# Gated unit of the experts: clamps moved to GpSimd, one eviction to ScalarE, the slots' small work rearranged

## The chip, the cores and the metric

One NeuronCore of a Trainium2 chip runs the program. The metric is the device time of one execution in microseconds (us); less is better.

## The reference

The reference is a whole small model on 512 tokens of width 1024: a first block (four token mixers, then 32 experts of which each token takes 4) and a second block of two layers. The change touches the experts alone. For one expert and its rows, with `w_gu` 1024 x 2048 and `w_down` 1024 x 1024, in fp32:

```
hg, hl = split(x @ w_gu[e] + b_gu[e])
hg = min(hg, 7);  hl = clip(hl, -7, 7)
y  = (hg * sigmoid(1.702 * hg) * (hl + 1)) @ w_down[e] + b_down[e]
out[token] += gate[token, e] * y
```

## The kernel before

The experts run one after the other (`for e in range(k.n_exp)`, up to L1538 and on). Each has 96 slots (`NS`): a token's rank in the expert is its slot. For each expert there are four steps.

**Slots** (`slots`, L1393 to L1414, called by `first`, L1468, two experts ahead). The narrow matrix `sel` (L1397) carries the bias rows. For each of the four groups of 128 tokens a one-hot matrix `o1` of 128 x 96 is made by comparing ranks with a row of slot numbers (VectorE, L1401), and a small matmul with it (L1402) puts token number, presence and gate of each slot into one PSUM tile. VectorE copies that to `sl` (L1404) and makes from it, in five operations on 96 x 1 elements (L1409 to L1413), the row `ix` to gather, the row `dx` to add to, and the gate `gc`.

**Rows** (`rows`, L1416, one expert ahead). GpSimd gathers the tokens' rows into `xg` by an indirect DMA (L1419). TensorE transposes them; `transposed` (L1224) evicts each transposed tile twice: ScalarE writes the high part (L1231), VectorE the low part (L1232).

**Main** (`main`, L1425). A fp32 product is made of three matmuls on split operands (high x high, high x low, low x high; L1148 to L1150). A weight piece of 128 x 2048 (1 MB) is loaded by SyncE's queue (L1204) into one of nine raw buffers; ScalarE copies it to the rounded high part `wh` (L1213), VectorE subtracts to get the low part `wl` (L1214). There are four buffers each of `wh` and `wl`. An expert has 12 pieces, eight for `w_gu` and four for `w_down`. The 2048 columns of `w_gu` are taken in two halves (`q`), each of which has a gate tile `pp[0]` and a linear tile `pp[1]` of 96 x 512 in PSUM, two pieces each. Once a half's tiles are there, the gated unit (L1440 to L1448) runs:

```
V.tensor_scalar(hg, pp[0], 7.0, None, op0=OP.min)
ACT.activation(sg, hg, AF.Sigmoid, scale=1.702)
V.tensor_scalar(hl, pp[1], 7.0, -7.0, op0=OP.min, op1=OP.max)
G.tensor_mul(hg, hg, sg)
V.scalar_tensor_tensor(hl, hl, 1.0, hg, op0=OP.add, op1=OP.mult)
last = transposed(hl, hT[0][:, 4 * q:4 * q + 4], hT[1][:, 4 * q:4 * q + 4])
```

(V is VectorE, ACT is ScalarE, G is GpSimd.) `hg`, `hl` and `sg` have one buffer each. The transposed `hT` (high part on ScalarE, low part on VectorE) is the operand of the down projection.

**Result.** ScalarE evicts the two halves of the product with the gate as scale (L1463), and GpSimd adds the rows to `h_d` by an indirect DMA (L1464, the scatter).

What runs in which order: each engine works its own queue strictly in order. The queues are laid out when the program is built, by the framework's planner, which goes through time in its own estimate of durations and takes for each engine what is ready there, earlier source lines first. So the order of a queue is not that of the source, and it changes when durations or dependences change. `issue_after` (used around the loads of the first experts and the extra work between experts) pins single orders; none of these lines is touched.

Of the kernel before, what the change touches and what calls it, by code (L numbers as in the profile page):

```python
# [8 lines left out]
F32 = mybir.dt.float32  # L9
F32R = mybir.dt.float32r  # L10
BF = mybir.dt.bfloat16
I32 = mybir.dt.int32
U32 = mybir.dt.uint32
AF = mybir.ActivationFunctionType
OP = mybir.AluOpType
# [5 lines left out]
NCH = 4  # L21
# [303 lines left out]
def tile_pool(tc, **kw):  # L325
    if kw.get("space") != bass.MemoryType.DRAM:
        kw["reuse_waits"] = "tile"
    return tc.tile_pool(**kw)
# [726 lines left out]
NS = 96  # L1055
# [90 lines left out]
def mm3(PE, out, a, b, start, stop):  # L1146

    PE.matmul(out, a[0], b[0], start=start, stop=False)  # L1148
    PE.matmul(out, a[0], b[1], start=False, stop=False)  # L1149
    PE.matmul(out, a[1], b[0], start=False, stop=stop)  # L1150


def block1_ffn(k, mix, wo, es_mix, b2):


    nc, tc, A = k.nc, k.tc, k.A
    V, ACT, G, PE = nc.vector, nc.scalar, nc.gpsimd, nc.tensor
    es, es_b, es_p, es_x = ExitStack(), ExitStack(), ExitStack(), ExitStack()
    with es:
# [7 lines left out]
        cons, sm = pool_x("fcons"), pool_x("sm")  # L1167
# [4 lines left out]
        iota, pidx = cst2[:, 0:128], cst2[:, 128:129]  # L1172
# [4 lines left out]
        Rm = cons.tile([128, NCH, N_EXP], F32, name="Rm")  # L1177
        aux = cons.tile([128, NCH, N_EXP, 6], BF, name="aux")
        dslot = cons.tile([128, 1], F32, name="dslot")
# [56 lines left out]
        with tile_pool(tc, name="w1", bufs=1) as w1:  # L1236
# [30 lines left out]
            eye3 = sm.tile([128, 32], F32, name="eye3")  # L1267
# [121 lines left out]


        with tile_pool(tc, name="ex", bufs=1) as ex:

            def slots(rm, ax, idc, eng=G):  # L1393


                sel = sm.tile([128, NS], BF, name="sel", bufs=3)
                eng.tensor_copy(sel, idc.to_broadcast([128, NS]))  # L1397
                pt = bank("tr", (NS, 512))
                for t in range(NCH):
                    o1 = sm.tile([128, NS], BF, name="o1", tag="o1", bufs=4)  # L1400
                    V.tensor_scalar(o1, iota[:, 0:NS], rm(t), None, op0=OP.is_equal)  # L1401
                    PE.matmul(pt[:, 0:6], o1, ax(t), start=t == 0, stop=t == NCH - 1)  # L1402
                sl = sm.tile([NS, 6], F32, name="sl", bufs=2)
                V.tensor_copy(sl, pt[:, 0:6])  # L1404
                tk = sm.tile([NS, 2], F32, name="tk", bufs=2)
                ix = sm.tile([NS, 1], I32, name="ix", bufs=3)
                dx = sm.tile([NS, 1], I32, name="dx", bufs=4)
                gc = sm.tile([NS, 1], F32, name="gc", bufs=4)
                V.scalar_tensor_tensor(tk[:, 0:1], sl[:, 1:2], 128.0, sl[:, 0:1], op0=OP.mult, op1=OP.add)  # L1409
                V.tensor_copy(ix, tk[:, 0:1])  # L1410
                V.tensor_scalar(tk[:, 1:2], sl[:, 2:3], -1.0, 1.0, op0=OP.mult, op1=OP.add)
                V.scalar_tensor_tensor(dx, tk[:, 1:2], dslot[:NS], tk[:, 0:1], op0=OP.mult, op1=OP.add)
                V.scalar_tensor_tensor(gc, sl[:, 3:4], sl[:, 4:5], sl[:, 5:6], op0=OP.add, op1=OP.add)  # L1413
                return sel, dx, gc, ix  # L1414

            def rows(sel, dx, gc, ix):  # L1416

                xg = ex.tile([NS, D], F32, name="xg", bufs=1)
                gathers.append(G.indirect_dma_start(out=xg, out_offset=None, in_=x1_d,  # L1419
                                                    in_offset=bass.IndirectOffsetOnAxis(ap=ix[:, :1], axis=0)))  # L1420
                xT = [ex.tile([128, 8, NS], F32R, name="xT%d" % i, bufs=2) for i in range(2)]
                transposed(xg, xT[0], xT[1])
                return sel, dx, gc, xT

            def main(st, wg, wd, mid=None, keep=None):  # L1425

                sel, dx, gc, xT = st
                hT = [ex.tile([128, 8, NS], F32R, name="hT%d" % i, bufs=1) for i in range(2)]
                for q in range(2):
                    pp = []  # L1430
                    for gl in range(2):
                        p = bank("gu", (NS, 512))
                        PE.matmul(p, sel, bias[:, 1024 * gl + 512 * q:1024 * gl + 512 * q + 512], start=True, stop=False)
                        for kh in range(2):
                            h, l = wg(4 * q + 2 * gl + kh)
                            for j in range(4):
                                a = 4 * kh + j
                                mm3(PE, p, (xT[0][:, a], xT[1][:, a]), (h[:, j], l[:, j]), False, a == 7)
                        pp.append(p)
                    hg = ex.tile([NS, 512], F32, name="hg", bufs=1)  # L1440
                    hl = ex.tile([NS, 512], F32, name="hl", bufs=1)
                    sg = ex.tile([NS, 512], F32, name="sg", bufs=1)
                    V.tensor_scalar(hg, pp[0], 7.0, None, op0=OP.min)
                    ACT.activation(sg, hg, AF.Sigmoid, scale=1.702)  # L1444
                    V.tensor_scalar(hl, pp[1], 7.0, -7.0, op0=OP.min, op1=OP.max)
                    G.tensor_mul(hg, hg, sg)  # L1446
                    V.scalar_tensor_tensor(hl, hl, 1.0, hg, op0=OP.add, op1=OP.mult)
                    last = transposed(hl, hT[0][:, 4 * q:4 * q + 4], hT[1][:, 4 * q:4 * q + 4])  # L1448
                with tc.issue_after(last.ins):
                    res = mid() if mid else None  # L1450
                y = None if keep else ex.tile([NS, D], F32, name="y", bufs=1)
                py = [bank("py", (NS, 512)) for _ in range(2)]
                for kh in range(2):
                    for n in range(2):
                        h, l = wd(2 * kh + n)
                        for j in range(4):
                            a = 4 * kh + j
                            mm3(PE, py[n], (hT[0][:, a], hT[1][:, a]), (h[:, j], l[:, j]), a == 0, a == 7)
                if keep:
                    keep(py, dx, gc)  # L1460
                    return res
                for n in range(2):
                    ACT.activation(y[:, 512 * n:512 * n + 512], py[n], AF.Copy, scale=gc)  # L1463
                G.indirect_dma_start(out=h_d, out_offset=bass.IndirectOffsetOnAxis(ap=dx[:, :1], axis=0),  # L1464
                                     in_=y, in_offset=None, compute_op=OP.add)
                return res

            first = lambda e: slots(lambda t: Rm[:, t, e:e + 1], lambda t: aux[:, t, e], eye3[:, e:e + 1], G if e else V)  # L1468
            def embedding():

                pe_ = xp.tile([128, NCH, D], F32, name="pe_", tag="x")
# [31 lines left out]
            def load_h(t):  # L1503
                nc.sync.dma_start(hs[t], h_d[128 * t:128 * t + 128])
# [27 lines left out]
            sl = [first(0)]  # L1532
# [21 lines left out]
            with tc.If(nov > 0):  # L1554
                with tc.For_i(0, nov, 1) as b:
                    e = nc.values_load(tble[0:1, bass.ds(b, 1)], min_val=0, max_val=N_EXP - 1)
                    rme = ex.tile([128, NCH, 1], F32, name="rme", bufs=1)
                    axe = ex.tile([128, NCH, 1, 6], BF, name="axe", bufs=1)
                    ide = ex.tile([128, 1], F32, name="ide", bufs=1)
                    jc = ex.tile([128, 1], F32, name="jc", bufs=1)  # L1560
                    V.tensor_copy(rme, Rm[:, :, bass.ds(e, 1)])
                    V.tensor_copy(axe, aux[:, :, bass.ds(e, 1)])
                    V.tensor_copy(ide, eye3[:, bass.ds(e, 1)])
                    V.tensor_copy(jc, tblj[:, bass.ds(b, 1)])
                    V.tensor_scalar(rme, rme, jc, None, op0=OP.subtract)
                    slow = lambda w: lambda i: unit(w[bass.ds(e, 1), i].rearrange("o p a b -> (o p) a b"), sx)
                    main(rows(*slots(lambda t: rme[:, t], lambda t: axe[:, t, 0], ide)), slow(A["wgu"]), slow(A["wdn"]))
                for t in range(2):
                    load_h(t)
            es_b.close()  # L1570
# [5 lines left out]
        with tile_pool(tc, name="pl", bufs=1) as pl:  # L1576
# [39 lines left out]
            for t in range(NCH):  # L1616
# [6 lines left out]
                for n in range(2):  # L1623
# [7 lines left out]
                    sg = pl.tile([128, 512], F32, name="sg", tag="sg", bufs=2)  # L1631
# [44 lines left out]
class B2:  # L1676
# [7 lines left out]
    def bank(self, tag, shape=(128, 512)):  # L1684
        n = int(np.prod(shape[1:]))
        a = self.ps.tile([128, 512], F32, name=tag, tag=tag, bufs={"gu": 4, "py": 2, "tr": 2}[tag])[:shape[0], :n]
        return a.rearrange("p (a b) -> p a b", a=shape[1]) if len(shape) == 3 else a
# [839 lines left out]
```

## Time and profile before

| | |
|---|---|
| median of 3 runs | 3156.93 us (3152.36 to 3159.75) |
| the profiled execution | 3154.36 us, its span 3152.6 us |
| busy share of the span | TensorE 94%, VectorE 68%, ScalarE 48%, GpSimd 26% |
| moved by the transfers | 582.12 MB, mean 185 GB/s |
| granted TensorE clock, mean | 0.968 |

The profile is one execution. Names: PE is TensorE's matmuls, PEld its weight loads, DVE is VectorE, ACT ScalarE, POOL GpSimd, SP SyncE (SPq its queue, which issues the loads). L1214 is line 1214 of the kernel. In a timeline the first column is the start in us from the span's start, the second the duration in us; `x2` after a line means two of the same merged, and the brackets hold the idle time ahead of the first and what ended it. The names of tiles are cut (`o` is `o1`). The experts lie between about 473 and 1690 us; before them are the mixers, after them the second block.

### The profile page before, as it was taken

Reading aid. Unit: us, or ns where it says so; the run is one execution under the profiler, and the core shown is the slowest. Engines: PE = TensorE matmul, PEld = TensorE weight load, DVE = VectorE, ACT = ScalarE, POOL = GpSimd, SP = SyncE. Lnnn points to the kernel's source line nnn. Section 1 sums busy time; section 2 is a strip of 40 time slices with the busy share of each in tenths; the row PEclk is TensorE's granted clock in tenths of the full one; section 3 lists DMA queues with packets and bytes.
Section 4 is the critical chain, followed back from the end, with each engine's and each line's share of the span. In section 5 each row is a group of like instructions: output and inputs, shape, how many; then the busy total and the mean of one; then the engine's idle time right before and its main releaser. Section 6 shows DMA issues by size and latency. Waiting matters only on the chain. (4 is left out here: it accounts for less than half of the span.)

```text
span 3152.6 us, 45612 instructions
## 1 busy us (share of the span) xinstructions
PE 2975.8 (94%) x18295; PEld 2471.6 (78%) x18295; DVE 2152.6 (68%) x3044; ACT 1521.8 (48%) x1838; POOL 831.8 (26%) x543
## 2 busy tenths in 40 slices
PE   6899879999999999999999999999999899999997
PEld 4799666666666666666666898999999799899997
DVE  4756679899999998899998756644233846834234
ACT  4421437776666666666665643342223534432222
POOL 1210333543333333233323310320103401310104
PEclk8999889999999999999999988999999999999998
DMA  3211368999999998899996211122222211232221
GB/s 122 74 35 35 109 248 324 342 369 351 350 351 346 348 351 323 336 341 345 349 350 226 79 58 41 57 91 82 93 94 80 97 41 46 76 108 87 99 78 52
DMA packets 106280, 582.12 MB, mean 185 GB/s; under 512 B 13080, under 2 KB 13736, under 8 KB 56048
## 3 DMA queue, kind: packets, MB, share of 16 engines
q1 hardware_dynamic: 94976, 541.12, 46.4%
q0 software_dynamic: 10896, 37.52, 4.5%
q8 instruction: 145, 2.38, 0.3%
q10 hardware_dynamic: 192, 0.52, 0.1%
q14 instruction: 71, 0.58, 0.1%
HBM read 560.17 MB, written 18.94 MB: 184 GB/s over the span
## 5 line engine op out<-in xcount | busy, mean ns | idle before, releaser
L1214 DVE TENSOR_TENSOR wl<-w,wh 128x2048 fp32r<-128x2048 f32 (+1 forms) x398 | 900.4, 2275 | 63.9 <-ACT wh L1213 63.7
L1213 ACT ACTIVATE wh<-w 128x2048 fp32r<-128x2048 f32 (+1 forms) x410 | 726.1, 1805 | 64.8 <-PE gu L1150 42.4
L1796 PE MATMUL gu<-hh,w 128*128 128x256 f32 (+2 forms) x1552 | 455.7, 294 | 10.4 <-ACT hh L2494 10.4
L1797 PE MATMUL gu<-hl,w 128*128 128x256 f32 (+2 forms) x1552 | 451.9, 291 | 2.0 <-DVE hl L2496 1.3
L1798 PE MATMUL gu<-hh,w 128*128 128x256 f32 (+2 forms) x1552 | 449.5, 290 | 1.8 <-DVE w L1142 1.8
L1149 PE MATMUL gu<-wl,xT 128*96 128x512 f32 x1024 | 416.8, 407 | 19.4 <-DVE wl L1214 18.5
L1148 PE MATMUL gu<-wh,xT 128*96 128x512 f32 x1024 | 410.8, 401 | 0.0
L1150 PE MATMUL gu<-wh,xT 128*96 128x512 f32 x1024 | 405.4, 396 | 0.0
L1142 DVE TENSOR_TENSOR w<-w 128x1024 fp32r<-128x1024 f32 (+1 forms) x190 | 237.6, 1251 | 238.0 <-ACT w L1141 237.8
L1141 ACT ACTIVATE w<-w 128x1024 fp32r<-128x1024 f32 (+1 forms) x194 | 201.2, 1038 | 259.8 <-PE gu L2320 84.6
L1796 PEld LDWEIGHTS gu<-hh,w 128*128 128x128 f32 x1552 | 301.4, 194 | 13.3 <-ACT hh L2494 12.0
L1797 PEld LDWEIGHTS gu<-hl,w 128*128 128x128 f32 x1552 | 300.0, 193 | 5.7 <-DVE hl L2496 3.9
L1798 PEld LDWEIGHTS gu<-hh,w 128*128 128x128 f32 x1552 | 300.8, 194 | 3.2 <-DVE w L1142 2.6
L1149 PEld LDWEIGHTS gu<-wl,xT 128*96 128x96 f32 x1024 | 165.5, 162 | 133.7 <-DVE wl L1214 70.7
L1446 POOL TENSOR_TENSOR hg<-hg,sg 96x512 f32<-96x512 f32 x64 | 170.8, 2669 | 284.8 <-ACT sg L1444 284.7
L2305 POOL TENSOR_TENSOR al<-fs,ah 128x528 fp32r<-128x528 f32 (+1 forms) x44 | 76.8, 1745 | 610.4 <-ACT ah L2304 610.4
L1148 PEld LDWEIGHTS gu<-wh,xT 128*96 128x96 f32 x1024 | 165.4, 162 | 69.5 <-ACT xT L1231 0.2
L1150 PEld LDWEIGHTS gu<-wh,xT 128*96 128x96 f32 x1024 | 165.7, 162 | 60.8
L1149 PE MATMUL py<-wl,hT 128*96 128x512 f32 x512 | 208.0, 406 | 1.8 <-DVE wl L1214 0.3
L1148 PE MATMUL py<-wh,hT 128*96 128x512 f32 x512 | 202.1, 395 | 1.7 <-ACT wh L1213 1.0
L1150 PE MATMUL py<-wh,hT 128*96 128x512 f32 x512 | 202.5, 398 | 0.0
L1464 POOL DMA_INDIRECT h_d<-y,dx x31 | 128.8, 4154 | 191.1 <-ACT y L1463 185.9
(707 smaller groups left out, 6413.7 us busy)
## 6 DMA issues: line engine op xcount, KB each, us to landing
w<-in_wgu SPq DMA_DIRECT2D x255, 1024.0 KB, 6.8
w<-in_wdn SPq DMA_DIRECT2D x127, 1024.0 KB, 7.6
w<-in_w SPq DMA_DIRECT2D x88, 512.0 KB, 4.3
w<-in_w2f SPq DMA_DIRECT2D x43, 512.0 KB, 4.6
w<-in_w22a SPq DMA_DIRECT2D x32, 512.0 KB, 4.4
w<-in_w1f SPq DMA_DIRECT2D x18, 512.0 KB, 3.6
w<-in_w2o SPq DMA_DIRECT2D x16, 512.0 KB, 4.3
w<-in_w22b SPq DMA_DIRECT2D x16, 384.0 KB, 4.3
```

What stands on the lines that cost most here:

```text
L1141: nc.scalar.activation(h, w, AF.Copy)
L1142: (eng or nc.vector).tensor_sub(l, w, h.bitcast(F32))
L1148: PE.matmul(out, a[0], b[0], start=start, stop=False)
L1149: PE.matmul(out, a[0], b[1], start=False, stop=False)
L1150: PE.matmul(out, a[1], b[0], start=False, stop=stop)
L1213: ACT.activation(h[:, j], w[:, j], AF.Copy)
L1214: (early or V).tensor_sub(l[:, j], w[:, j], h[:, j].bitcast(F32))
L1446: G.tensor_mul(hg, hg, sg)
L1464: G.indirect_dma_start(out=h_d, out_offset=bass.IndirectOffsetOnAxis(ap=dx[:, :1], axis=0), in_=y, in_offset=None, compute_op=OP.add)
L1796: PE.matmul(p, w[0][:, kk], x[0][:, kk, c], start=kk == ks[0], stop=False)
L1797: PE.matmul(p, w[0][:, kk], x[1][:, kk, c], start=False, stop=False)
L1798: PE.matmul(p, w[1][:, kk], x[0][:, kk, c], start=False, stop=kk == ks[-1])
```

## The change

The gate branch: ScalarE takes the sigmoid straight from PSUM; GpSimd limits the result from above with the constant sigmoid(1.702 x 7), made once in `smax` (the sigmoid is monotone, so this equals the sigmoid of the clamped value); VectorE clamps the PSUM value and multiplies in one operation. The linear branch: ScalarE copies the PSUM tile to SBUF, GpSimd clamps it on both sides in place, VectorE's last product stays. In the slots, one operation compares all four groups (`o1` has one buffer now, of 4 x 96); the matmuls read its quarters. For all experts but the first, `sl` is evicted by ScalarE and the five narrow operations run on GpSimd.

```diff
@@ -1389,6 +1389,9 @@
 
 
         with tile_pool(tc, name="ex", bufs=1) as ex:
+            smax = sm.tile([128, 1], F32, name="smax", bufs=1)
+            G.memset(smax, 7.0)
+            ACT.activation(smax, smax, AF.Sigmoid, scale=1.702)
 
             def slots(rm, ax, idc, eng=G):
 
@@ -1396,21 +1399,25 @@
                 sel = sm.tile([128, NS], BF, name="sel", bufs=3)
                 eng.tensor_copy(sel, idc.to_broadcast([128, NS]))
                 pt = bank("tr", (NS, 512))
+                o1 = sm.tile([128, NCH, NS], BF, name="o1", tag="o1", bufs=1)
+                V.tensor_tensor(o1, iota[:, 0:NS][:, None, :].to_broadcast([128, NCH, NS]),
+                                rm.to_broadcast([128, NCH, NS]), op=OP.is_equal)
                 for t in range(NCH):
-                    o1 = sm.tile([128, NS], BF, name="o1", tag="o1", bufs=4)
-                    V.tensor_scalar(o1, iota[:, 0:NS], rm(t), None, op0=OP.is_equal)
-                    PE.matmul(pt[:, 0:6], o1, ax(t), start=t == 0, stop=t == NCH - 1)
+                    PE.matmul(pt[:, 0:6], o1[:, t], ax(t), start=t == 0, stop=t == NCH - 1)
                 sl = sm.tile([NS, 6], F32, name="sl", bufs=2)
-                V.tensor_copy(sl, pt[:, 0:6])
+                if eng is V:
+                    V.tensor_copy(sl, pt[:, 0:6])
+                else:
+                    ACT.activation(sl, pt[:, 0:6], AF.Copy)
                 tk = sm.tile([NS, 2], F32, name="tk", bufs=2)
                 ix = sm.tile([NS, 1], I32, name="ix", bufs=3)
                 dx = sm.tile([NS, 1], I32, name="dx", bufs=4)
                 gc = sm.tile([NS, 1], F32, name="gc", bufs=4)
-                V.scalar_tensor_tensor(tk[:, 0:1], sl[:, 1:2], 128.0, sl[:, 0:1], op0=OP.mult, op1=OP.add)
-                V.tensor_copy(ix, tk[:, 0:1])
-                V.tensor_scalar(tk[:, 1:2], sl[:, 2:3], -1.0, 1.0, op0=OP.mult, op1=OP.add)
-                V.scalar_tensor_tensor(dx, tk[:, 1:2], dslot[:NS], tk[:, 0:1], op0=OP.mult, op1=OP.add)
-                V.scalar_tensor_tensor(gc, sl[:, 3:4], sl[:, 4:5], sl[:, 5:6], op0=OP.add, op1=OP.add)
+                eng.tensor_scalar(tk[:, 0:1], sl[:, 1:2], 128.0, sl[:, 0:1], op0=OP.mult, op1=OP.add)
+                eng.tensor_copy(ix, tk[:, 0:1])
+                eng.tensor_scalar(tk[:, 1:2], sl[:, 2:3], -1.0, 1.0, op0=OP.mult, op1=OP.add)
+                eng.tensor_scalar(dx, tk[:, 1:2], dslot[:NS], tk[:, 0:1], op0=OP.mult, op1=OP.add)
+                eng.tensor_scalar(gc, sl[:, 3:4], sl[:, 4:5], sl[:, 5:6], op0=OP.add, op1=OP.add)
                 return sel, dx, gc, ix
 
             def rows(sel, dx, gc, ix):
@@ -1440,10 +1447,12 @@
                     hg = ex.tile([NS, 512], F32, name="hg", bufs=1)
                     hl = ex.tile([NS, 512], F32, name="hl", bufs=1)
                     sg = ex.tile([NS, 512], F32, name="sg", bufs=1)
-                    V.tensor_scalar(hg, pp[0], 7.0, None, op0=OP.min)
-                    ACT.activation(sg, hg, AF.Sigmoid, scale=1.702)
-                    V.tensor_scalar(hl, pp[1], 7.0, -7.0, op0=OP.min, op1=OP.max)
-                    G.tensor_mul(hg, hg, sg)
+
+                    ACT.activation(sg, pp[0], AF.Sigmoid, scale=1.702)
+                    G.tensor_scalar(sg, sg, smax[:NS], None, op0=OP.min)
+                    V.scalar_tensor_tensor(hg, pp[0], 7.0, sg, op0=OP.min, op1=OP.mult)
+                    ACT.activation(hl, pp[1], AF.Copy)
+                    G.tensor_scalar(hl, hl, 7.0, -7.0, op0=OP.min, op1=OP.max)
                     V.scalar_tensor_tensor(hl, hl, 1.0, hg, op0=OP.add, op1=OP.mult)
                     last = transposed(hl, hT[0][:, 4 * q:4 * q + 4], hT[1][:, 4 * q:4 * q + 4])
                 with tc.issue_after(last.ins):
@@ -1465,7 +1474,7 @@
                                      in_=y, in_offset=None, compute_op=OP.add)
                 return res
 
-            first = lambda e: slots(lambda t: Rm[:, t, e:e + 1], lambda t: aux[:, t, e], eye3[:, e:e + 1], G if e else V)
+            first = lambda e: slots(Rm[:, :, e:e + 1], lambda t: aux[:, t, e], eye3[:, e:e + 1], G if e else V)
             def embedding():
 
                 pe_ = xp.tile([128, NCH, D], F32, name="pe_", tag="x")
@@ -1564,7 +1573,7 @@
                     V.tensor_copy(jc, tblj[:, bass.ds(b, 1)])
                     V.tensor_scalar(rme, rme, jc, None, op0=OP.subtract)
                     slow = lambda w: lambda i: unit(w[bass.ds(e, 1), i].rearrange("o p a b -> (o p) a b"), sx)
-                    main(rows(*slots(lambda t: rme[:, t], lambda t: axe[:, t, 0], ide)), slow(A["wgu"]), slow(A["wdn"]))
+                    main(rows(*slots(rme, lambda t: axe[:, t, 0], ide)), slow(A["wgu"]), slow(A["wdn"]))
                 for t in range(2):
                     load_h(t)
             es_b.close()
```

## Rows read from the trace of the kernel before

**Rows 1.** Busy time in stretches of 38.70 us: engine (instructions), granted clock, DMA share, GB/s

```profile
677.40:716.10 38.70, 38.34 (x179) 26.57 (x178) 38.48 (x35) 28.56 (x23) 15.88 (x5) 1.00 0.99 371
...
832.20:870.90 38.70, 37.76 (x170) 25.03 (x171) 35.43 (x33) 26.02 (x20) 13.21 (x5) 1.00 0.97 354
```

**Rows 2.** Timeline of DVE, 842 to 881 us: start, duration, operation

```profile
842.21 0.27 DVE L1401 TENSOR_SCALAR o<-fcst,Rm 128x96 bf16<-128x96 f32 x1 [0.55 <-PE tr L1402]
...
843.10 2.28 DVE L1214 TENSOR_TENSOR wl<-w,wh 128x2048 fp32r<-128x2048 f32 x1
...
851.27 0.69 DVE L1443 TENSOR_SCALAR hg<-gu 96x512 f32<-96x512 f32 x1 [0.66 <-PE gu L1150]
851.88 2.28 DVE L1214 TENSOR_TENSOR wl<-w,wh 128x2048 fp32r<-128x2048 f32 x1
854.53 2.93 DVE L1214 TENSOR_TENSOR wl<-w,wh 128x2048 fp32r<-128x2048 f32 x1 [0.37 <-ACT wh L1213]
857.38 0.68 DVE L1445 TENSOR_SCALAR hl<-gu 96x512 f32<-96x512 f32 x1
858.17 0.69 DVE L1447 SCALAR_TENSOR_TENSOR hl<-hl,hg 96x512 f32<-96x512 f32 x1
...
862.07 2.29 DVE L1214 TENSOR_TENSOR wl<-w,wh 128x2048 fp32r<-128x2048 f32 x1 [0.54 <-ACT wh L1213]
864.28 0.68 DVE L1443 TENSOR_SCALAR hg<-gu 96x512 f32<-96x512 f32 x1
...
880.59 0.27 DVE L1401 TENSOR_SCALAR o<-fcst,Rm 128x96 bf16<-128x96 f32 x1 [0.57 <-PE tr L1402]
```

**Rows 3.** Timeline of PEld (weight loads), from 870.60 us on

```profile
870.60 0.16 PEld L1150 LDWEIGHTS py<-wh,hT 128*96 128x96 f32 x1
870.83 0.16 PEld L1148 LDWEIGHTS py<-wh,hT 128*96 128x96 f32 x1
...
871.98 0.54 PEld L1230 LDWEIGHTS tr<-fcst,hl 96*128 96x128 f32 x4
872.46 0.16 PEld L1150 LDWEIGHTS py<-wh,hT 128*96 128x96 f32 x1
```

**Rows 4.** Waits, 600 to 1600 us: us in total, times, longest

```profile
ACT hT L1231 <- PE tr L1230: 152.7, 47, 4.6
...
ACT sg L1444 <- DVE hg L1443: 80.9, 46, 3.1
PEld gu L1149 <- DVE wl L1214: 64.7, 108, 1.7
```

**Rows 5.** Timeline of ACT, 852 to 864 us

```profile
852.06 0.63 ACT L1444 ACTIVATE sg<-hg 96x512 f32<-96x512 f32 x1 [2.81 <-DVE hg L1443]
852.60 3.71 ACT L1213 ACTIVATE wh<-w 128x2048 fp32r<-128x2048 f32 x2
859.74 0.49 ACT L1231 ACTIVATE hT<-tr 128x384 fp32r<-128x384 f32 x1 [3.44 <-PE tr L1230]
860.13 3.71 ACT L1213 ACTIVATE wh<-w 128x2048 fp32r<-128x2048 f32 x2
```

**Rows 6.** Timeline of POOL, 846 to 855 us

```profile
846.52 5.45 POOL L1464 DMA_INDIRECT h_d<-y,dx  x1 [0.30 <-issue]
852.77 2.54 POOL L1446 TENSOR_TENSOR hg<-hg,sg 96x512 f32<-96x512 f32 x1 [0.81 <-ACT sg L1444]
```

**Rows 7.** Single lines on POOL: ns min/median/max, first and last start us, forms

```profile
L1446 POOL TENSOR_TENSOR hg<-hg,sg x64: 1287/2547/7555, 477.5 to 1685.1; 96x512 f32<-96x512 f32 x64
...
L1397 POOL CAST sel<-eye x31: 262/267/4967, 402.3 to 1542.2; 128x96 bf16<-128x96 f32 x31
...
L528 POOL MEMSET SC<- x1: 529/529/529, 4.7 to 4.7; 128x512 f32 x1
```

**Rows 8.** Groups by line, 600 to 1600 us: count, busy us, mean ns, idle before

```profile
L1401 DVE TENSOR_SCALAR o<-fcst,Rm 128x96 bf16<-128x96 f32 x104 | 35.0, 370 | 9.0 <-PE tr L1402 9.0
...
L1480 ACT ACTIVATE pe__10029<-gu 128x512 f32<-128x512 f32 x8 | 4.8, 595 | 9.5 <-PE gu L1150 9.5
```

**Rows 9.** Transfers: a 10 us stretch (columns as rows 1), and SPq's waits, 600 to 1600

```profile
1310.00:1320.00 10.00, 9.70 (x47) 6.57 (x46) 9.70 (x8) 5.48 (x5) 0.00 (x0) 1.00 1.02 423
...
SPq L1204 <- DVE wl L1214: 844.9, 301, 12.3
```

## The prediction

> **What bounds the kernel now.** I read the busy time by stretches first, because the change touches one stage, the 32 experts from about 473 to 1690 us. Each row of [rows 1] is 38.70 us, about one expert. In the later one TensorE shows 37.76 us busy, VectorE 35.43, ScalarE 26.02, and the transfers 0.97; no engine has the stage to itself, but VectorE and TensorE are both nearly full. The next expert is a copy of it: the pair of one-hot operations that starts at 842.21 starts again at 880.59 [rows 2], so one expert takes 38.38 us.
>
> TensorE's own work is less. A triple of matmuls shows weight loads 0.23 us apart, and four transposes push the next load back by about half a microsecond [rows 3]. One expert has 12 weight pieces of 12 matmuls, four bias matmuls and 16 transposes: 144 x 0.23 + 4 x 0.23 + 4 x 0.5 = 36.0 us. The other 2.4 us are bubbles; 64.7 us of waits in 1000 us stand against VectorE's low parts "wl" [rows 4]. So 2.4 us an expert, some 75 us over 31 experts, is the most that any relief of the helpers can bring before TensorE itself is the bound.
>
> Why does VectorE come late when it is not full? Its stretch from 851.27 to 864.28 is one half of an expert, 13.01 us [rows 2], and with ScalarE's queue beside it [rows 5] it reads as a closed chain: clamp "hg" 851.27, sigmoid 852.06, weight copy 852.60, low part "wl" 854.53, clamp "hl" 857.38, product 858.17, transposes on TensorE, eviction hT 859.74, weight copy 860.13, low part 862.07, and the next clamp at 864.28. The steps are 0.79 + 0.54 + 1.93 + 2.85 + 0.79 + 1.57 + 0.39 + 1.94 + 2.21 = 13.01. TensorE needs 48 x 0.23 + 2 x 0.23 + 0.5 = 12.0 for a half. ScalarE waits in its queue for hT while weight copies stand behind it: that wait, 152.7 us, is the largest of an engine that matters, and the one for "hg" is 80.9 [rows 4]. The chain through ScalarE's in-order queue, not VectorE's sum, sets the half.
>
> GpSimd is idle most of the time, yet not free to use: its product of two tiles of 512 elements takes 2.54 us at 852.77 [rows 6], against a minimum of 1.29 [rows 7]. It starts while VectorE's low part of 851.88 runs, ends 1.15 us after that has ended, and the next low part takes 2.93 instead of 2.28 [rows 2]. The two take turns: GpSimd waits for a VectorE operation on two SBUF tiles, then holds the next one up by 0.65. A one-operand cast does the same: 0.26 us at best, 4.97 at worst [rows 7].
>
> **The change, part by part.** *Gate branch.* The sigmoid no longer waits for VectorE's clamp: the link of 0.79 drops from the chain, and ScalarE's weight copy with it comes 0.7 us earlier. The clamp by GpSimd and the product on VectorE follow off the chain, but the product, 0.69 by the one at 858.17 [rows 2], takes the place that the clamp had in VectorE's queue, and what stands behind it (the low part that TensorE wants next) waits if GpSimd is late. GpSimd is late if the scatter of the previous expert's result is still there, 5.45 us from 846.52 [rows 6]: it ended at 851.97, 0.1 us before the sigmoid began at 852.06 [rows 5]. Cover is thus thin once per expert.
>
> *Linear branch.* VectorE's clamp, a link of 0.79, becomes an eviction by ScalarE, 0.60 by the nearest row [rows 8], with 0.07 to its semaphore, then a GpSimd clamp and another semaphore of 0.1. *A clamp on GpSimd* does not occur in this trace with one operand on 96x512. From below I bound it by the fill of 128x512, 0.53, which reads nothing, from above by the two-operand minimum of 1.29 [rows 7]; I take 0.8, nearer to the fill because one operand is read instead of two. The linear link is then 0.67 + 0.9 = 1.57 instead of 0.79. [...]
>
> Per half, with the order of the queues kept, the chain is 13.01 - 0.79 + 0.78, plus up to 0.6 where the gate's product now stands ahead of a low part: 13.0 to 13.6, no gain.
>
> *VectorE's load.* One operation of 0.6 goes per half, and the 0.65 of being held up goes; two clamps of 0.8 now take turns with its low parts. That is -1.25 + 1.6, no relief worth the name: GpSimd's work is paid in VectorE's time where the clamps meet low parts.
>
> *Slots.* Four one-hots become one of 384 elements, and six narrow operations leave VectorE. From 842.21 to 843.10 two one-hots and the six narrow ones take 0.89 [rows 2]; the other two one-hots take half of 0.74, the mean of one being 0.37 [rows 8]. One operation of 4 x 96 costs 0.27 to 0.69 (one narrow one-hot up to the 512-element product), I take 0.45. So VectorE gets back 0.8 us per expert. What it loses is five narrow GpSimd operations at 0.1 to 0.26 each; at worst each is held up by a low part, 5 x 2.28 = 11.4 us of GpSimd's queue, ahead of gather and scatter. The gather it feeds is one expert ahead, so this costs nothing unless it pushes the scatter past the sigmoid as above; then the price is at most the 2 to 3 us by which the gate's clamp is late. ScalarE gains an eviction of 96x6, 0.2, in slack. The single one-hot buffer and the constant at the start are worth nothing each.
>
> **Where the gain comes from.** The chain closes only because hT stands in ScalarE's queue ahead of the second pair of weight copies (859.74 before 860.13). The new hT becomes ready 0.8 us later; the queue order is fixed when the program is built, in order of estimated readiness, so I expect the planner to put one more weight copy ahead of hT, and its low part ahead of the hT low part on VectorE. Then 0.39 + 1.94 + 2.21 no longer follow the transposes, the chain is open, and TensorE's 12.0 per half binds. With VectorE as full as before I take half of the 1.0: 0.5 x 62 halves = 31 us, and 5 us for the slots: 36 us. Against the profiled execution's 3154.4 that is 3118; the median of the runs is 2.6 above, so **3121 us**. The same sum at a clamp of 1.29 loses 2 x 0.49 x 62 = 61 at worst, at 0.53 it gains up to 33; with half of either on the path, this case alone spans 3090 to 3150.
>
> **Rivals.** *TensorE fully fed:* 2.4 x 31 = 74 us, 3083. For it: between 677.40 and 716.10 the transfers ran at 371 GB/s and TensorE was 38.34 us busy of 38.70 [rows 1]. Against: VectorE was 38.48 busy there, and its load does not fall.
>
> *The order stays, or the clamps simply move the time:* 13.0 for 13.01, nothing measurable (under 0.2%, about 6 us, cannot be told from no change): 3157. For it: the turns that GpSimd and VectorE take.
>
> *Slower, by the linear clamp held up.* If the planner lets the next low part run while ScalarE evicts the second branch, the clamp waits for it, up to 2.28 us, as the product did at 852.77, and the transposes, hT and what stands behind hT come that much later. If a weight copy that TensorE needs is still behind hT, the half is about 15 us: 2.1 x 62 = 130, 3287; if that holds in one half of each expert, 3222. It decides when the hold exceeds the 1.0 us of slack per half. For it: the product met a low part in nearly every half (median 2.55 against 1.29 [rows 7]); against: the planner sees the longer chain.
>
> *The transfers bind.* In the repeating expert the loads move 354 GB/s with a share of 0.97 [rows 1]; if that is all they give, an expert stays at 38.4 us and nothing is gained: 3157. Against: 371 GB/s over a whole such stretch [rows 1], 423 over 10 us, and the loads wait 844.9 us of 1000 for low parts that free their buffers [rows 9]; they follow, they don't lead. [...]
>
> **Chances.** Forecast 0.44, fully fed 0.08 (faster, 0.52 together); transfers 0.03 and no net change 0.14 (same, 0.17); slower 0.31. The range runs from the fully fed 3080 to 3205, which takes in the cheap part of the slower case; the likeliest case's own range is 3090 to 3150.
>
> **What would show it.** Right: ScalarE's wait for the transposes of hT well under 152.7 us in the same 1000 us, three or more weight copies between sigmoid and hT, VectorE waiting more for GpSimd but TensorE less for "wl", an expert in about 37.2 us. Step by step: one-operand clamps of 0.5 to 1.3 us when not held up, one one-hot near 0.45. Wrong: clamps of 2.5 us and above between ScalarE's eviction and the second product, with waits of TensorE for "wl" grown; or a product of the gate that stands waiting behind the scatter, with low parts late behind it.

## The result, and the profile after

The changed kernel takes 3246.69 us (median of 4, 3233.50 to 3257.98) against 3158.34 for the kernel before: a ratio of 1.0278, 95% interval 1.0246 to 1.0311. It is slower by 88 us, outside the range of the prediction.

The profiled execution took 3242.62 us, 88.3 more than that of before. Between the first and the last gate operation of VectorE lie 1297.3 us, where 1210.5 lay before; so nearly all of it, 86.8 us, is in the experts, some 2.8 us an expert. The first rows are VectorE's timeline of the changed kernel, two experts.

```profile
969.46 0.56 DVE L1403 TENSOR_TENSOR o<-fcst,Rm 128x384 bf16<-128x384 f32 x1 [0.95 <-PE tr L1406]
...
972.61 4.49 DVE L1214 TENSOR_TENSOR wl<-w,wh 128x2048 fp32r<-128x2048 f32 x2
980.98 0.69 DVE L1453 SCALAR_TENSOR_TENSOR hg<-gu,sg 96x512 f32<-96x512 f32 x1 [3.88 <-POOL sg L1452]
981.59 4.48 DVE L1214 TENSOR_TENSOR wl<-w,wh 128x2048 fp32r<-128x2048 f32 x2
986.57 0.69 DVE L1456 SCALAR_TENSOR_TENSOR hl<-hl,hg 96x512 f32<-96x512 f32 x1 [0.51 <-POOL hl L1455]
...
990.53 2.29 DVE L1214 TENSOR_TENSOR wl<-w,wh 128x2048 fp32r<-128x2048 f32 x1 [0.60 <-ACT wh L1213]
994.28 0.69 DVE L1453 SCALAR_TENSOR_TENSOR hg<-gu,sg 96x512 f32<-96x512 f32 x1 [1.46 <-POOL sg L1452]
...
1009.74 0.56 DVE L1403 TENSOR_TENSOR o<-fcst,Rm 128x384 bf16<-128x384 f32 x1 [0.95 <-PE tr L1406]
...
1051.42 0.56 DVE L1403 TENSOR_TENSOR o<-fcst,Rm 128x384 bf16<-128x384 f32 x1 [0.96 <-PE tr L1406]
```

One expert takes 40.28 us, the next 41.68, where [rows 2] had 38.38. In the first of them VectorE stands still twice for the gate's product: 3.88 us in the first half, 1.46 in the second. What it waits for is in GpSimd's timeline:

```profile
970.12 3.51 POOL L1473 DMA_INDIRECT h_d<-y,dx  x1 [7.50 <-ACT y L1472]
973.17 3.97 POOL L1416 TENSOR_SCALAR tk<-sl 96x1 f32<-96x1 f32 x1
977.11 0.18 POOL L1418 TENSOR_SCALAR tk<-sl 96x1 f32<-96x1 f32 x1
977.29 0.38 POOL L1420 TENSOR_SCALAR gc<-sl 96x1 f32<-96x1 f32 x1
977.63 0.18 POOL L1417 CAST ix<-tk 96x1 int32<-96x1 f32 x1
977.79 0.33 POOL L1419 TENSOR_SCALAR dx<-tk,dslot 96x1 int32<-96x1 f32 x1
978.28 1.02 POOL L1426 DMA_INDIRECT xg<-x_d,ix  x1 [0.16 <-POOL dx L1419]
979.36 1.59 POOL L1452 TENSOR_SCALAR sg<-sg,smax 96x512 f32<-96x512 f32 x1
981.32 5.22 POOL L1455 TENSOR_SCALAR hl<-hl 96x512 f32<-96x512 f32 x1 [0.37 <-ACT hl L1454]
991.08 3.17 POOL L1452 TENSOR_SCALAR sg<-sg,smax 96x512 f32<-96x512 f32 x1 [4.54 <-ACT sg L1451]
```

Read the two together. An operation on one element per partition (973.17) takes 3.97 us: it ends when VectorE's two low parts end, at 977.10. From there VectorE has nothing in front of the gate's product and waits until 980.98, in the order of its queue: the weight copies for the two low parts behind the product (975.65, 3.70 us for both) have ended by 979.35. Meanwhile GpSimd works off its queue: four narrow operations, the gather, and last the clamp of the sigmoid, which takes 1.59 us. The sigmoid itself was ready since 975.75, as ScalarE's timeline shows. In the second half nothing stands ahead of the clamp: it starts at 991.08 beside the low part of 990.53, takes 3.17 us instead of 1.59, and ends 1.43 us after that low part.

```profile
975.16 0.59 ACT L1451 ACTIVATE sg<-gu 96x512 f32<-96x512 f32 x1 [1.27 <-PE gu L1150]
975.65 3.70 ACT L1213 ACTIVATE wh<-w 128x2048 fp32r<-128x2048 f32 x2
980.64 0.59 ACT L1454 ACTIVATE hl<-gu 96x512 f32<-96x512 f32 x1 [1.28 <-PE gu L1150]
981.13 1.90 ACT L1213 ACTIVATE wh<-w 128x2048 fp32r<-128x2048 f32 x1
988.20 0.49 ACT L1231 ACTIVATE hT<-tr 128x384 fp32r<-128x384 f32 x1 [5.17 <-PE tr L1230]
```

Three weight copies stand between sigmoid and hT, one more than in [rows 5]. The planner did reorder as forecast. The waits of the same 1000 us as [rows 4], and after them the last of these lines in the kernel before:

```profile
ACT hT L1231 <- PE tr L1230: 196.0, 48, 7.6
DVE hg L1453 <- POOL sg L1452: 127.1, 48, 3.9
...
PEld gu L1149 <- DVE wl L1214: 64.1, 49, 3.5
...
PE gu L1149 <- DVE wl L1214: 33.4, 18, 3.1
```

```profile
PE gu L1149 <- DVE wl L1214: 17.9, 54, 1.3
```

ScalarE's wait for hT rose from 152.7 to 196.0; VectorE has a new one, 127.1 in 24 experts. TensorE's waits for "wl" are fewer than before and longer: those of its weight loads add up to the same (64.1 us against 64.7 [rows 4], but 49 times, not 108), those of its matmuls to nearly twice as much. After some of them the matmuls are slower, too. Here are TensorE's matmuls after the long wait of the first expert (983.92) and of the second, which takes 41.68 us:

```profile
983.92 0.48 PE L1149 MATMUL gu<-wl,xT 128*96 128x512 f32 x1 [1.82 <-DVE wl L1214]
...
1024.18 0.74 PE L1149 MATMUL gu<-wl,xT 128*96 128x512 f32 x1 [1.82 <-DVE wl L1214]
1024.72 0.63 PE L1150 MATMUL gu<-wh,xT 128*96 128x512 f32 x1
1025.14 0.63 PE L1148 MATMUL gu<-wh,xT 128*96 128x512 f32 x1
...
1027.72 0.39 PE L1149 MATMUL gu<-wl,xT 128*96 128x512 f32 x1
1027.95 0.39 PE L1150 MATMUL gu<-wh,xT 128*96 128x512 f32 x1
```

```profile
984.00:988.00 4.00, 4.00 (x21) 2.84 (x21) 3.49 (x3) 0.00 (x0) 2.54 (x1) 1.00 1.00 353
1024.00:1028.00 4.00, 3.82 (x11) 2.58 (x12) 3.49 (x4) 0.00 (x0) 2.80 (x1) 0.60 0.97 350
```

After the second wait some seven matmuls start 0.43 us apart instead of 0.23: the granted clock is 0.50 from 1024.20 to 1027.20, and 0.60 on average between 1024 and 1028 (columns as in [rows 1]). After the first, as long, it stays at 1.00. Seven times 0.2 is 1.4 us, the difference of the two experts. From 860 to 1310 us the trace goes on in this way: experts of some 40.3 and 41.7 us take turns, and a stretch of lower granted clock lies in every second one: over 4 us it is 0.58 from 860, 0.74 from 940, 0.60 from 1024, 0.72 from 1104, 0.62 from 1188 and 0.70 from 1268.

### The profile page after: what moved, and what is told of

Same layout as the page of the kernel before. It is cut to its first block, busy times and chain, and to the rows that moved or that the text cites. A ratio compares the mean times of both kernels' runs of the same rounds, so it can differ in the third digit from the quotient of the medians.

```text
span 3240.8 us, 45635 instructions
## 1 busy us (share of the span) xinstructions
PE 2977.8 (92%) x18295; PEld 2485.6 (77%) x18295; DVE 2053.7 (63%) x2698; ACT 1568.4 (48%) x1943; POOL 1102.8 (34%) x763
## 5 line engine op out<-in xcount | busy, mean ns | idle before, releaser
L1214 DVE TENSOR_TENSOR wl<-w,wh 128x2048 fp32r<-128x2048 f32 (+1 forms) x398 | 866.9, 2201 | 70.7 <-ACT wh L1213 69.9
L1149 PE MATMUL gu<-wl,xT 128*96 128x512 f32 x1024 | 423.8, 414 | 40.0 <-DVE wl L1214 39.8
L1148 PE MATMUL gu<-wh,xT 128*96 128x512 f32 x1024 | 422.9, 413 | 0.0
L1150 PE MATMUL gu<-wh,xT 128*96 128x512 f32 x1024 | 411.1, 401 | 0.0
L1455 POOL TENSOR_SCALAR hl<-hl 96x512 f32<-96x512 f32 x64 | 231.3, 3614 | 111.3 <-ACT hl L1454 111.0
L1148 PEld LDWEIGHTS gu<-wh,xT 128*96 128x96 f32 x1024 | 170.2, 166 | 73.2 <-issue 1.1
L1150 PEld LDWEIGHTS gu<-wh,xT 128*96 128x96 f32 x1024 | 171.9, 168 | 68.1 <-issue 1.2
L1473 POOL DMA_INDIRECT h_d<-y,dx x31 | 92.5, 2985 | 294.7 <-ACT y L1472 264.6
```

Of the source, the lines that this page charges most:

```text
L1214: (early or V).tensor_sub(l[:, j], w[:, j], h[:, j].bitcast(F32))
L1455: G.tensor_scalar(hl, hl, 7.0, -7.0, op0=OP.min, op1=OP.max)
```

## The experiments

Three theories stood at the start. **G:** the gate's product waits in VectorE's queue for GpSimd. **L:** the linear clamp, held up by low parts (5.22 us at 981.32), delays hT; this was the rival of the prediction. **S:** the narrow slot work on GpSimd makes everything late. All ratios are against the kernel before, in runs beside it.

| kernel | us | ratio, 95% interval |
|---|---|---|
| changed | 3246.69 | 1.0278 (1.0246 to 1.0311) |
| gate branch as before | 3185.88 | 1.0085 (1.0055 to 1.0114) |
| linear branch as before | 3257.82 | 1.0287 (1.0241 to 1.0333) |
| slots as before | 3234.86 | 1.0229 (1.0187 to 1.0271) |
| narrow work on VectorE | 3232.10 | 1.0223 (1.0202 to 1.0244) |
| limit as one constant | 3253.13 | 1.0289 (1.0254 to 1.0324) |
| limit as two constants | 3194.70 | 1.0102 (1.0072 to 1.0131) |
| clamp done, not read | 3161.11 | 0.9986 (0.9973 to 1.0000) |
| no limit | 3118.65 | 0.9867 (0.9834 to 0.9900) |
| gate branch alone changed | 3213.51 | 1.0150 (1.0114 to 1.0186) |
| linear branch and one-hot alone | 3155.07 | 0.9998 (0.9977 to 1.0019) |
| one-hot alone | 3161.90 | 0.9997 (0.9981 to 1.0013) |
| nothing of the gated unit on GpSimd | 3135.05 | 0.9908 (0.9879 to 0.9936) |
| limit in the last product | 3114.15 | 0.9852 (0.9820 to 0.9884) |
| the same, narrow work on VectorE | 3123.54 | 0.9879 (0.9847 to 0.9911) |

**The gate put back.**

```diff
-ACT.activation(sg, pp[0], AF.Sigmoid, scale=1.702)
-G.tensor_scalar(sg, sg, smax[:NS], None, op0=OP.min)
-V.scalar_tensor_tensor(hg, pp[0], 7.0, sg, op0=OP.min, op1=OP.mult)
+V.tensor_scalar(hg, pp[0], 7.0, None, op0=OP.min)
+ACT.activation(sg, hg, AF.Sigmoid, scale=1.702)
...
+G.tensor_mul(hg, hg, sg)
```

> The changed kernel with the gate branch alone as before (VectorE clamps, ScalarE takes the sigmoid, GpSimd multiplies); the linear branch and the slots stay changed. Theory G (VectorE's new product stands first in its queue and waits for GpSimd's clamp of the sigmoid, 127.1 us in 1000, 5.3 us per expert): the wait is gone and most of the 88 us come back, 3150 to 3180 us. Theory L (the linear clamp, held up by low parts, delays hT and the weight copies behind it): the linear branch is untouched, so 3220 to 3260 us, with the wait of hT for the transposes still near 8 us per expert. Theory S (the narrow slot work on GpSimd is what makes everything late): some 3200 us or more, since GpSimd's queue stays as long.

Measured 3185.88, just above G's span: 61 us come back of 88, and L's 3220 or more is excluded. The planner lays the queues of VectorE and ScalarE out in another order here, so this run does not change one thing alone.

**The linear branch put back.**

```diff
-ACT.activation(hl, pp[1], AF.Copy)
-G.tensor_scalar(hl, hl, 7.0, -7.0, op0=OP.min, op1=OP.max)
+V.tensor_scalar(hl, pp[1], 7.0, -7.0, op0=OP.min, op1=OP.max)
```

> The changed kernel with the linear branch alone as before (VectorE clamps from PSUM); gate and slots stay changed. Theory G: VectorE still waits 4 to 6 us per expert for the clamp of the sigmoid, and it has 1.2 us per expert more to do: 3220 to 3280 us. Theory L: the held-up clamp is gone, hT comes earlier, 3140 to 3180 us. Theory S: little changes, 3220 to 3260 us.

3257.82: nothing comes back, so L falls. The clamp of 5.22 us is long, but VectorE works through two low parts meanwhile and waits 0.51 us for it.

**The slots put back** (the lines of `slots` as before), and **the narrow work alone on VectorE** (`eng` replaced by `V` in the six narrow operations).

> The changed kernel with the slots as before (four one-hots and the six narrow operations on VectorE); both branches of the gated unit stay changed. Theory S: GpSimd's queue is clear when the sigmoid comes, the time falls to 3150 to 3180 us. Theory G: the clamp itself still takes 1.6 us where nothing holds it up, so VectorE waits some 1.5 us in both halves, 3 us per expert instead of 5.3; with 0.8 us per expert given back to VectorE, 3190 to 3220 us. Theory L: 3230 to 3270 us.

> The changed kernel with the narrow slot operations alone on VectorE (eviction of 96x6 too); the one-hot stays one operation, both branches stay changed. It takes the 3.97 us of the first narrow operation and some 1.1 us of the others out of GpSimd's queue ahead of the first half's clamp. Theory S: 3150 to 3180 us. Theory G: the first half's wait falls from 3.9 to about 1.5 us, a gain of at most 2.4 x 31 = 74 us, less 0.5 us per expert on VectorE: 3180 to 3210 us. Theory L: no gain, 3235 to 3265 us.

3234.86 and 3232.10. That is 12 and 15 us less than the changed kernel, the first within the intervals: much less than S claims, and less than G did in both. The wait is not gone but changed: with GpSimd's queue shorter by the narrow work, the planner puts gather and scatter directly ahead of the clamp, and the first half still waits 3.05 us. This is the clamp in the run with the narrow work on VectorE, and the product that waits for it:

```profile
963.09 2.49 POOL L1426 DMA_INDIRECT xg<-x_d,ix  x1 [8.66 <-issue]
965.88 5.08 POOL L1473 DMA_INDIRECT h_d<-y,dx  x1 [0.30 <-ACT wh L1213]
970.47 2.12 POOL L1452 TENSOR_SCALAR sg<-sg,smax 96x512 f32<-96x512 f32 x1
972.63 0.69 DVE L1453 SCALAR_TENSOR_TENSOR hg<-gu,sg 96x512 f32<-96x512 f32 x1 [3.05 <-POOL sg L1452]
```

**How long the clamp is.** The limit as a constant, then as two.

```diff
-G.tensor_scalar(sg, sg, smax[:NS], None, op0=OP.min)
+G.tensor_scalar(sg, sg, 0.999993304, None, op0=OP.min)            # one constant
+G.tensor_scalar(sg, sg, 0.999993304, 0.0, op0=OP.min, op1=OP.max) # two constants
```

> The changed kernel with the limit of the sigmoid as a constant in GpSimd's instruction instead of a tile of one value per partition; nothing else. The clamp of the linear branch, which has constants, took 0.61 us at best, the clamp of the sigmoid 1.55. Theory G with the duration of the clamp as its larger part: clamp near 0.6, VectorE's waits for it down by about 0.9 us per half, so 1.9 x 31 = 58 us less at most: 3190 to 3220 us. Theory Q (the clamp is late because of what stands ahead of it in GpSimd's queue and of the low part that runs, its own duration is minor): 3230 to 3255 us.

> The changed kernel with the limit of the sigmoid as two constants (minimum, then maximum with 0, which changes nothing of a sigmoid). In the run with one constant the clamp still took 1.48 us at best; the clamp of the linear branch, with two operations, takes 0.61. If the second operation is what selects the fast form, the clamp takes 0.6 us, VectorE's waits fall by 0.9 us in each half, 5.2 to 3.4 us per expert: theory G with the clamp's duration 3175 to 3215 us; theory Q (its place in GpSimd's queue) 3225 to 3255. If it stays at 1.5 us, 3240 to 3260.

The clamp's line in the changed kernel, in the run with one constant and in that with two (ns min/median/max), and VectorE's wait in the last of them:

```profile
L1452 POOL TENSOR_SCALAR sg<-sg,smax x64: 1548/1587/4777, 478.7 to 1774.4; 96x512 f32<-96x512 f32 x64
```

```profile
L1452 POOL TENSOR_SCALAR sg<-sg x64: 1481/1507/4765, 488.8 to 1791.7; 96x512 f32<-96x512 f32 x64
```

```profile
L1452 POOL TENSOR_SCALAR sg<-sg x64: 602/608/3850, 493.4 to 1731.0; 96x512 f32<-96x512 f32 x64
...
DVE hg L1453 <- POOL sg L1452: 86.5, 50, 2.9
```

Whether the limit comes from a tile hardly matters; a second operation that does nothing brings 1.5 us down to 0.6. The time falls with it, to 3194.70, the middle of what G expected of the clamp's duration, and VectorE's wait in the 1000 us from 127.1 to 86.5. The run with one constant had fitted Q in its time, but it had not shortened the clamp; the one with two falls out of Q's span. In a steady expert the queues of VectorE, ScalarE and GpSimd have the same order as in the changed kernel, so a new order is not the cause. The duration of the clamp alone carries over 50 us of the loss.

**The clamp done but not read.** GpSimd clamps into a tile `s2` that nothing reads; the limit is missing in the result.

> The changed kernel in which GpSimd still clamps the sigmoid, into a tile of its own that nothing reads; VectorE's product takes the unclamped sigmoid, so the limit is left out of the result. GpSimd has all the work of the changed kernel and takes its turns with VectorE's low parts; VectorE does not wait for it. Theory G (the wait of the product in VectorE's queue): 3115 to 3160 us. Theory P (GpSimd's work itself, by the turns that it and VectorE take): 3200 to 3250 us.

```profile
984.00 0.56 DVE L1403 TENSOR_TENSOR o<-fcst,Rm 128x384 bf16<-128x384 f32 x1 [0.95 <-PE tr L1406]
...
991.54 0.68 DVE L1454 SCALAR_TENSOR_TENSOR hg<-gu,sg 96x512 f32<-96x512 f32 x1
...
1000.39 0.69 DVE L1457 SCALAR_TENSOR_TENSOR hl<-hl,hg 96x512 f32<-96x512 f32 x1 [3.76 <-POOL hl L1456]
...
1021.90 0.56 DVE L1403 TENSOR_TENSOR o<-fcst,Rm 128x384 bf16<-128x384 f32 x1 [0.95 <-PE tr L1406]
```

3161.11, just above G's span: with all its work still on GpSimd, and the same order of the queues in a steady expert, 85 us go when VectorE does not wait for it. So the wait carries the loss against the kernel before. P's 3200 is excluded, but P is not nothing: the time is that of the kernel before and no less, and the second product now waits 3.76 us.

**No limit.** The clamp's line is left out.

> The changed kernel without the limit on the sigmoid; for a gate value above 7 the product then uses the sigmoid of the unclamped value, which is left out here. VectorE's product waits for ScalarE alone. Theory G: VectorE's wait falls from 5.3 us to under 1 us per expert and more comes back than in the run with the gate branch as before (3186), since ScalarE no longer waits for a clamp either: 3120 to 3180 us. If 3200 or more, the wait was a symptom.

3118.65, faster than the kernel before by 1.3%. VectorE's timeline has an expert of 36.43 us:

```profile
961.27 0.56 DVE L1403 TENSOR_TENSOR o<-fcst,Rm 128x384 bf16<-128x384 f32 x1 [0.95 <-PE tr L1406]
...
968.82 0.68 DVE L1452 SCALAR_TENSOR_TENSOR hg<-gu,sg 96x512 f32<-96x512 f32 x1
969.42 4.48 DVE L1214 TENSOR_TENSOR wl<-w,wh 128x2048 fp32r<-128x2048 f32 x2
976.18 0.69 DVE L1455 SCALAR_TENSOR_TENSOR hl<-hl,hg 96x512 f32<-96x512 f32 x1 [2.28 <-POOL hl L1454]
...
997.70 0.56 DVE L1403 TENSOR_TENSOR o<-fcst,Rm 128x384 bf16<-128x384 f32 x1 [0.95 <-PE tr L1406]
```

The gate's product starts without a wait. The second product still waits for GpSimd in the first half, 2.28 us, and that is hidden: over 400 us TensorE is busy for 395.90. The 42 us between this run and the one with the unread clamp are the price of that clamp in GpSimd's queue: there the linear clamp stood behind it, and the second product waited 1.48 us longer in the first half (3.76 against 2.28), about as much as the expert is longer (37.90 against 36.43). VectorE's waits for the linear clamp in 1000 us, there and here:

```profile
DVE hl L1457 <- POOL hl L1456: 92.5, 52, 4.6
...
DVE hl L1455 <- POOL hl L1454: 62.3, 54, 3.6
```

**Single parts.** The gate branch alone changed; the linear branch and the one-hot alone (gate as before, narrow work on VectorE); the one-hot alone; nothing of the gated unit on GpSimd (no limit, linear clamp and narrow work on VectorE).

> The kernel before with the gate branch alone changed (sigmoid from PSUM, GpSimd clamps it, VectorE's product waits for that); linear branch and slots as before. Theory G: VectorE waits 1.5 us in one half and 3 us in the half with the scatter ahead, as in the run with the slots as before: 3225 to 3265 us, slower than before by as much as the whole change. If the loss needs the longer queue on GpSimd (slots or linear clamp), 3160 to 3200 us.

> The changed kernel with the gate branch as before and the narrow slot work on VectorE: what is left of the change is the linear branch (ScalarE evicts, GpSimd clamps) and the one one-hot operation. If the narrow operations ahead of GpSimd's product and clamp cost the 23 us that stayed when the gate was put back: 3155 to 3170 us. If the linear branch itself costs them: 3180 to 3195.

> The kernel before with one one-hot operation of 384 elements for four of 96, nothing else changed in substance (the narrow work stays on VectorE, both branches as before). Saves about 0.72 - 0.48 = 0.25 us of VectorE per expert by start-to-start times, 8 us in all if it is on the chain: 3150 to 3163 us. If the single buffer makes it wait for TensorE, slower by up to 1 us per expert, 3190.

> No clamp and no product on GpSimd: ScalarE takes the sigmoid from PSUM, VectorE clamps and multiplies in one operation, VectorE clamps the linear branch from PSUM as before; one one-hot operation, narrow slot work on VectorE. The limit on the sigmoid is left out. VectorE has as many operations of 512 elements as before, but GpSimd takes no turns with its low parts (0.65 us per half), ScalarE's sigmoid comes 0.7 us earlier, and the slots save 0.4 us per expert. Theory G: up to the 2.4 us of bubbles per expert come back against the kernel before: 3085 to 3135 us. If VectorE's sum is what binds, 3140 to 3160.

The gate branch alone costs 1.5%, 3213.51, between the two spans that were expected: less than G's, so the other parts deepen the wait (102.1 us in 1000 for the gate's product, 127.1 with all of them), and more than the other's. The linear branch and the one-hot together give and cost nothing that can be told, and the one-hot alone neither. The run with the linear branch and the one-hot differs from the one with the gate put back only by the narrow work, which is on VectorE in it: so on GpSimd, with the old product behind it, the narrow work cost 0.9%. Off GpSimd altogether the kernel is 0.9% faster than before, at the edge of what G expected.

**A version that is faster than both.** x sigmoid(1.702 x) grows with x for positive x, so the limit on x can be a limit on the product, which the last operation of VectorE takes in place of adding 1; ScalarE adds the 1 while it evicts.

```diff
+ACT.activation(sg, pp[0], AF.Sigmoid, scale=1.702)
+V.tensor_tensor(hg, pp[0], sg, op=OP.mult)
+ACT.activation(hl, pp[1], AF.Copy, bias=1.0)
+G.tensor_scalar(hl, hl, 8.0, -6.0, op0=OP.min, op1=OP.max)
+V.scalar_tensor_tensor(hl, hg, 6.999953128, hl, op0=OP.min, op1=OP.mult)
```

> The whole function without a clamp on GpSimd in the gate branch: VectorE multiplies the gate value with its sigmoid, and the last product takes the minimum of that and 7 sigmoid(11.914) (the product grows with the gate value there, so the limit on the product is the limit on the value). The 1 of the linear branch is added by ScalarE's eviction, GpSimd clamps to -6 and 8. As many instructions on each engine as in the run without the clamp, which took 3118.65. Theory G: 3110 to 3130 us. If the planner orders the queues differently, up to 3160.

> The kernel with the limit in the last product (3114.15) with the narrow slot work on VectorE instead of GpSimd. If the narrow work on GpSimd hurts only because the clamp of the gate stands behind it: no gain, VectorE has 0.5 us per expert more, 3114 to 3130 us. If it hurts by itself (the linear clamp behind it, VectorE's second product late in the first half): 3085 to 3108 us.

3114.15: 1.5% under the kernel before, with nothing left out. With the narrow work on VectorE it is 3123.54, no gain, the intervals overlap. The second product waits for the linear clamp in the first half of an expert, in the faster run and in the other:

```profile
971.53 0.69 DVE L1452 SCALAR_TENSOR_TENSOR hl<-hg,hl 96x512 f32<-96x512 f32 x1 [2.29 <-POOL hl L1451]
...
984.14 0.69 DVE L1452 SCALAR_TENSOR_TENSOR hl<-hg,hl 96x512 f32<-96x512 f32 x1 [0.51 <-POOL hl L1451]
```

So the narrow work on GpSimd makes VectorE wait longer for the linear clamp behind it, and that costs nothing here; it cost where the clamp or the product of the gate stood behind it. Busy times over 400 us of the faster one (columns as in [rows 1]):

```profile
800.00:1200.00 400.00, 396.51 (x1848) 274.21 (x1847) 347.14 (x232) 298.79 (x254) 197.77 (x111) 1.00 0.98 368
```

## Why the prediction was wrong, point by point

- *A chain through ScalarE's queue sets the half, TensorE's 36.0 us per expert is the floor.* It fits: with three weight copies ahead of hT and the gate free, the expert takes 36.43 us. No run opens that chain and changes nothing else.
- *The planner puts one more weight copy ahead of hT.* Right, in the changed kernel itself.
- *Gate branch.* **This step failed.** It said that the product "takes the place that the clamp had in VectorE's queue" and that what stands behind it waits if GpSimd is late, and then charged "up to 0.6" and, for the scatter, 2 to 3 us that entered neither the sum nor the rivals; such a product stood only among the signs of being wrong. VectorE needed the result of the old product on GpSimd 2.86 us after its end (855.31 in [rows 6], 858.17 in [rows 2]); it needs the new clamp's 1.35 us after the sigmoid (975.75 to 977.10), before the clamp has begun, for an operation ahead of two low parts. The wait is 3.88 + 1.46 = 5.34 us an expert. It did not need an unlucky scatter, which here ended before the sigmoid began: in the first half GpSimd got no turn until VectorE had run out of low parts, so that the other four narrow operations, the gather and the clamp began (977.11) just when VectorE had nothing left to cover them (977.10); in the second the clamp itself was held up by a low part, 3.17 us for 1.59.
- *A clamp of 0.8 between 0.53 and 1.29.* The term was mis-sized in the gate: 1.59 us, outside the bounds that I took for safe, and worth over 50 us by the run with two operations. The linear clamp at 0.61 lay inside.
- *The narrow slot work "costs nothing unless it pushes the scatter past the sigmoid".* Wrong in place: it stood, with the gather, between the scatter and the clamp, 1.1 and 1.0 us of the first half's wait. With nothing of the gate behind it, it costs nothing, as the last pair of runs shows (3114.15 with it on GpSimd, 3123.54 without). The five operations took 0.18 to 0.40 us at best, for the 0.1 to 0.26 that I had put down without a row for the 0.1, and ScalarE's eviction 0.17 for 0.2. The one one-hot took 0.56 us for the 0.45 taken, and gave nothing.
- *The rival "slower"* had the right sign, and the time lies between its two prices (3222 and 3287), but at the wrong place: the linear clamp took 5.22 us where 0.61 is its best, held up longer than thought, without deciding anything.
- *The transfers.* They did not bind: that rival took the 354 GB/s of the steady expert [rows 1] for all that they give, and the faster version moved 368 over 400 us.
- *The number.* The predicted 3121 us is near what the kernel does without the clamp of the gate (3118.65), but that is in part luck. The sum had a clamp in it, and with the clamp done and only the wait taken away the kernel takes 3161.11: none of the 36 us of gain is there. That is what the rival had in which "the clamps simply move the time" (3157). So two things were missing: the wait of the gate's product, worth 85 us, and the clamp's place ahead of the linear clamp in GpSimd's queue, worth some 40.
- *The range.* Half of the 33 us that a clamp of 0.53 would gain leads from 3121 to 3104; no term leads to the 3090 that was given. And the upper end of 3205 left out both prices of the rival "slower", though it had a chance of 0.31.

## What to carry to other kernels

When work moves from one engine's queue to another's, ask of each consumer not only how much less it has to do, but when it now needs the result. Here the old product took 2.54 us on GpSimd and was done 2.86 us before its use: VectorE waited for it 4.5 us in 1000. The new clamp takes 1.59 us, is needed at once and puts what stands ahead of it in GpSimd's queue onto VectorE: 127.1 us in 1000. In the first half GpSimd's work was not hidden behind VectorE's low parts: four narrow operations, the gather and the clamp began (977.11) when they had stopped (977.10). And a limit, a scale or a 1 can often be folded into an operation that runs anyway: that was worth 4% here between two ways of writing the same clamp.

## What the runs showed of the hardware

- On GpSimd the same scalar operation on 96x512 took at best 1.48 us (limit as a constant) and 1.55 (limit from a tile) with one operation (minimum), and 0.60 with two (minimum, maximum). The 0.8 of the prediction lies between the two forms.
- In the changed kernel GpSimd got no turn between two low parts of VectorE that followed each other at once: an operation on 96x1 that took 0.40 at best took 3.97, and every GpSimd operation of the experts (the issues of transfers aside) that began beside the first of two such low parts ended behind the second. In [rows 6] the product did get in, where VectorE had a gap of 0.37 us. It is not so everywhere: with the clamp unread, a cast on 96x1 began at 992.15 with the first of two low parts (992.14, 4.48 us for both), took 2.32 us and so ended between them. Nor was VectorE's next low part always held up, as by 0.65 us in [rows 2]: in the kernel before, beside the cast of 4.97 us [rows 7], which began at 638.28, the three low parts from 638.64 on took 6.75 us together.
- TensorE's wait of 1.82 us for a low part was followed, in every second expert from 860 to 1310 us, by matmuls at a lower granted clock (0.50 from 1024.20 to 1027.20), 1.4 us more for that expert. A wait as long, before 983.92, was not: 1.00 up to 988. What decides between the two is not shown. The kernel before had a granted clock of 1.00 over 800 to 1200 us, and one such stretch up to 1310 us, 0.50 from 1260 to 1264.
